# A hybrid decoder step: the first norm done by halves of the features, with the first products over the first half between

## The chip, the cores and the metric

The kernel runs on one core of a Trainium2 chip. The metric is the device time of one execution in microseconds (us), lower is better; a kernel's time is the median of several executions. A profile is one execution recorded by the hardware. The engines are PE (matrix products; PEld is its weight load), DVE (VectorE), ACT (ScalarE), POOL (GpSimd) and SP, which in this kernel only issues loads and stores. Each engine works through its own list of instructions in order.

## The reference

The kernel computes one step of a decoder of two layers, for 256 prompt tokens and 8 samples of 4 tokens, 288 tokens in all, with 1024 features. Layer 0 mixes by a gated delta rule, layer 1 by a Mamba-2 scan; each mixer is followed by a feed-forward block. All of this case happens ahead of the first mixer:

```python
cs = jax.nn.silu(c)                                   # 9 rows: one for the prompt, one for each sample
mod = cs @ p['w_mod'][i] + p['b_mod'][i]              # 1024 x 6144 weights per layer
sh1, sc1, gt1, sh2, sc2, gt2 = [m[:, None, :] for m in jnp.split(mod, 6, axis=-1)]
h = _rmsnorm(x, p['norm_mix'][i]) * (1 + sc1) + sh1   # x * rsqrt(mean(x*x) + eps) * weight
...
proj = h @ w_in                                       # q, k, v, z, and 32 columns beta_raw, a_raw
g = -exp(a_log) * softplus(a_raw + dt_bias)
cum = jnp.cumsum(g, axis=-1)                          # in chunks of 64 tokens
```

The outputs are the tokens after both layers and a final norm, and the states of the two mixers.

## The kernel before

Features lie on the partitions, in 8 tiles of 128 (index k), tokens along the free axis (288). Products are exact to fp32: activations and weights are each split into a high and a low part (`hh` and `hl`; `wh` and `wl`), and each feature tile takes three matmuls of 128x288: hh with wh, hh with wl, hl with wh. For weights, ACT makes `wh` as a copy with rounding and DVE makes `wl` as the difference (`chunk_load`, L267); a chunk is 4 feature tiles by 256 columns, 512 KB.

Loaded fp32 weights go through a pool of six tiles of 512 KB, tag "raw" (`raw_tile`, L141). It serves the conditioning weights and the product weights alike and is used in turn: a load takes the buffer of the sixth tile before it, and waits until the readers of that one are done. `wh` has four buffers and `wl` two. All loads are issued on SP in the order of its list.

The conditioning (`mod_steps`, L147) takes one slice of 1024 columns of w_mod in 8 loads of 128 rows. After every second load comes a burst of 8 matmuls, in which four column groups share one PSUM tile; after the last one ACT copies the sums (`mt`), PE transposes them in two pieces (`pt`), and DVE adds the bias and, for a scale, multiplies with the norm's weight (`modT`). A list `todo` holds all slices; `fill` and `ensure` take so many loads from it, and later stages weave the rest in between their work (`mods(8)` beside the first projections).

At the start (main body, L1584 on) the order is: c; two loads of w_mod; the bias and the norm weights; three tiles of x, with two loads of w_mod behind each of the first two; four loads more. Each x tile is transposed on PE and copied by DVE. Then comes the norm: ACT squares the tiles, DVE sums them (`acc`), two matmuls with ones give the mean (`ss`), ACT turns it into `rs` by a logarithm and an exponential, and DVE multiplies (`xr`). Constants of the convolutions and final norms (vr1 to vr3) are loaded and transposed. `ensure(2)` completes the slices of scale and shift, `load32` brings the 32 columns of beta and a, and `Norm.apply` makes `hh` and `hl`: first the 32 sample columns of all tiles (`hs`), then tile by tile a DVE step with scale and shift, an ACT copy to `hh` and a DVE difference to `hl`.

The mixer (`gdn`, L544) then computes the 32 columns (`dense32`, result `ba`), transposes them (`pb`), and forms beta and g: `gb` needs the bias `dtb`, which ACT's queue loads; softplus is an exponential on ACT (`spe`) and a row of small DVE steps (`spq`, `spp`); then `g`, and `pb` again as the cumulated sums, products with `triU`. Beside it run the projections of q and k by pairs of 128 columns (`k_pair`, L750; `dense_g`, L297): 48 matmuls a pair, evacuated by ACT (`ext`), followed by the convolution on DVE (`cva`, L72), and `kf`.

The order of each engine's list is fixed when the kernel is built, by a scheduler that works from the program's order and priorities.

Of the kernel before, what the change touches and what calls it, by code (L numbers as in the profile page):

```python
# [27 lines left out]
def tile_hybrid_step(ctx: ExitStack, tc: tile.TileContext, I, O):  # L28
# [45 lines left out]
    def tt(out, a, b, op):  # L74
        V.tensor_tensor(out=out, in0=a, in1=b, op=op)  # L75
# [99 lines left out]

    mod = {(l, s): const.tile([P, KD, 9], F32, name=f"modT{l}{s}") for l in range(2) for s in range(6)}
# [23 lines left out]
    class Norm:  # L200
# [22 lines left out]
        def apply(self, A, B, u=None, W=None, c0=0, at=()):  # L223

            r = None if u is not None else self.rstd()
            t = sqt("hs")[:, 0:256].rearrange("p (k t) -> p k t", k=KD)
            t4 = t.rearrange("p k (b t) -> p k b t", t=4)
            xs = (x if u is None else u)[:, :, NP_:NT].rearrange("p k (b t) -> p k b t", t=4)
            bc = lambda a: a[:, :, 1:9].unsqueeze(3).to_broadcast([P, KD, NB, 4])
            tt(t4, xs, bc(A), MUL)  # L230
            if u is None:
                tt(t, t, r[:, NP_:NT].unsqueeze(1).to_broadcast([P, KD, NS]), MUL)
            tt(t4, t4, bc(B), ADD)
            cp(hh[:, :, NP_:NT], t)
            tt(hl[:, :, NP_:NT], t, hh[:, :, NP_:NT].bitcast(F32), SUB)
            for k in range(KD):
                for i, a_ in enumerate(at):
                    if a_ == k:
                        load_early(W, c0, 4 * i, 4)
                if u is None:  # L240
                    v = sqt("hu")[:, 0:NP_]
                    stt(v, x[:, k, 0:NP_], A[:, k, 0:1], r[:, 0:NP_], MUL, MUL)
                    h = act(hh[:, k, 0:NP_], v, AF.Identity, bias=B[:, k, 0:1])
                    last = stt(hl[:, k, 0:NP_], v, B[:, k, 0:1], hh[:, k, 0:NP_].bitcast(F32), ADD, SUB)
                else:
                    v = u[:, k, 0:NP_]
                    ts(v, v, A[:, k, 0:1], B[:, k, 0:1], MUL, ADD)
                    cp(hh[:, k, 0:NP_], v)
                    tt(hl[:, k, 0:NP_], v, hh[:, k, 0:NP_].bitcast(F32), SUB)
            if u is None:  # L250
                self.after = [h, last]
# [123 lines left out]

    def dense32(W, c0, xh, xl):
        ps = psd.tile([P, NT], F32, tag="d", name="pd")
        whv, wlv = early.pop((c0, 32), None) or load32(W, c0)
        for k in range(KD):
            mm(ps, whv[:, k, :], xh[:, k, :], start=(k == 0), stop=False)  # L380
            mm(ps, wlv[:, k, :], xh[:, k, :], start=False, stop=False)
            mm(ps, whv[:, k, :], xl[:, k, :], start=False, stop=(k == KD - 1))
        return ps
# [160 lines left out]
    def gdn(gt1, nrm):  # L544
# [19 lines left out]
        pba = dense32(W, 6144, hh, hl)  # L564
# [168 lines left out]
        with tc.tile_pool(name="gp1", bufs=1) as p1:  # L733
# [17 lines left out]
            def k_pair(p_):  # L751
                ps = []
                yield from dense_g(ps, W, 1024 + p_ * 256, KD, hh, hl)
# [826 lines left out]
    queue_mods(0, (1, 0, 2, 3, 4, 5))  # L1580
    queue_mods(1, range(6))
    nrm = Norm()
    with tc.tile_pool(name="boot", bufs=1) as bp:
# [3 lines left out]
        act(cin, cin, AF.Silu)  # L1587
        pc = pm([P, KD, 32], "pc")
# [3 lines left out]
        fill(2)  # L1592
# [5 lines left out]
        for i, n in enumerate((P, P, NS)):  # L1598
            t = bp.tile([P, DM], F32, name=f"xt{i}")
            src = I["x_prompt"][0, i * P:(i + 1) * P, :] if i < 2 else I["x_sample"].rearrange("b t d -> (b t) d")  # L1600
            SY.dma_start(t[:n], src)
# [5 lines left out]
            if i < 2:  # L1607
                fill(2)
# [3 lines left out]
        fill(4)  # L1612
# [4 lines left out]
        for k in range(KD):  # L1617
            tt(xr[:, k, :], x[:, k, :], r, MUL)
        SY.dma_start(vr[1], I["gdn_conv_w"].rearrange("o w (r c) -> (o w r) c", c=P))
# [19 lines left out]
    nrm.apply(sc2, sh2, None, I["ffn_w_gate_up"][0], 0, (0,))  # L1639
# [40 lines left out]
    nrm.apply(sc1, sh1, None, I["ssm_w_in"][0], 4096, (0,))  # L1680
    nrm = Norm()
    ssm(gt1, nrm)
    nrm.apply(sc2, sh2, None, I["ffn_w_gate_up"][1], 0, (4,))
# [73 lines left out]
```

## Time and profile before

| | us |
|---|---|
| median of 3 runs | 1190.71 (1189.5 to 1194.89) |
| the profiled execution | 1194.17 |
| its span, first to last instruction | 1192.5 |
| PE busy | 1120.5 (94%) |
| DVE busy | 857.2 (72%) |
| ACT busy | 617.5 (52%) |
| DMA, mean over the span | 209 GB/s |

The mean granted clock of PE in the profiled execution was 0.972 of full speed. Times of the trace count from the span's start. In a chain of waits each row is a piece of the path that ended last, followed back from the last instruction. In a timeline a row gives start, length, engine, line, operation, output and inputs, and in brackets how long the engine had been idle and which instruction ended that. A group's row gives its count, busy time, mean ns of one, and the idle time ahead of it.

### The profile page before, as it was taken

The page shows a single profiled execution, that of the slowest core. Times are in us where ns is not written, and L with a number is a line of the kernel's source. Part 1 is how long each engine was busy: PE and PEld are TensorE (multiplying, and loading weights), DVE is VectorE, ACT ScalarE, POOL GpSimd, SP SyncE. Part 2 cuts the span into 40 slices and gives each one's busy share as a digit, 9 for nine tenths or more (in the row PEclk, how much of TensorE's full clock was granted, in tenths as well). Part 3 has the DMA queues.
Part 4 walks back from the last instruction along what each step waited for, and adds up shares of the span by engine and source line. Part 5 has one row for each costly group of instructions (what it writes and reads, how often), then busy time and mean ns, then how long its engine had stood idle before and what let it go on. Part 6 is the DMA issues. An engine that isn't in the chain of part 4 may idle for free.

```text
span 1192.5 us, 23174 instructions
## 1 busy us (share of the span) xinstructions
PE 1120.5 (94%) x8550; PEld 1022.6 (86%) x8550; DVE 857.2 (72%) x2080; ACT 617.5 (52%) x1315; POOL 120.9 (10%) x323
## 2 busy tenths in 40 slices
PE   5899999999989989999999899989979999999996
PEld 3689777798979879999999788768859899999996
DVE  2887897888767777666665777667876686666654
ACT  3587335555444464434343666887833484444432
POOL 3111104112100210100000111000000110000000
PEclk8999999899989989999999899999989989999998
DMA  8866696543354669888765767676464679887771
GB/s 301 258 205 179 187 290 189 174 150 105 103 173 152 206 205 315 271 273 266 240 196 157 255 204 235 192 226 202 147 208 146 190 227 302 256 254 232 216 215 51
DMA packets 270000, 249.04 MB, mean 209 GB/s; under 512 B 13314, under 2 KB 256247, under 8 KB 269888
## 3 DMA queue, kind: packets, MB, share of 16 engines
q1 hardware_dynamic: 269256, 247.51, 67.0%
q8 instruction: 67, 1.10, 0.4%
q14 instruction: 45, 0.37, 0.1%
q10 hardware_dynamic: 632, 0.07, 0.0%
HBM read 226.64 MB, written 20.90 MB: 208 GB/s over the span
## 4 chain that ended last, share of the span: by engine, by line
PE 72%; DVE 11%; DMA 8%; ACT 5%; issue 2%; POOL 1%; SPq 0%; DVEq 0%; ACTq 0%; POOLq 0%
PE pd L62 55%; PE pch L62 4%; DVE cva L72 3%; PE mod L62 3%; DVE wl L75 2%; DMA wm<-in_w_mod_dram 2%; DMA rw<-in_ssm_w_in_dram 1%; DMA rw<-in_gdn_w_in_dram 1%; ACT wh L87 1%; DMA D<-scumd 1%; PE py L62 1%; ACT D L82 1%; PE lsu L62 1%; PE pht L1431 1%; DMA rw<-in_gdn_w_out_dram 1%
## 5 line engine op out<-in xcount | busy, mean ns | idle before, releaser
L62 PE MATMUL pd<-hh,wh 128*128 128x288 f32 x1424 | 430.9, 305 | 13.8 <-ACT hh L87 10.4
L62 PE MATMUL pd<-hh,wl 128*128 128x288 f32 x1424 | 428.9, 302 | 4.6 <-DVE wl L75 4.3
L62 PE MATMUL pd<-hl,wh 128*128 128x288 f32 x1424 | 424.7, 300 | 1.2 <-DVE hl L72 1.0
L75 DVE TENSOR_TENSOR wl<-rw,wh 128x1024 fp32r<-128x1024 f32 (+2 forms) x258 | 310.7, 1204 | 153.7 <-PE pd L62 108.8
L87 ACT ACTIVATE wh<-rw 128x1024 fp32r<-128x1024 f32 (+2 forms) x258 | 268.1, 1041 | 251.5 <-PE pd L62 151.7
L62 PEld LDWEIGHTS pd<-hh,wh 128*128 128x128 f32 x1424 | 270.4, 191 | 27.5 <-issue 14.1
L62 PEld LDWEIGHTS pd<-hh,wl 128*128 128x128 f32 x1424 | 271.1, 190 | 11.0 <-DVE wl L75 8.1
L62 PEld LDWEIGHTS pd<-hl,wh 128*128 128x128 f32 x1424 | 270.4, 190 | 3.4 <-DVE hl L72 1.5
L62 PE MATMUL pd<-ah,wh 128*128 128x288 f32 x352 | 104.6, 297 | 0.0
L62 PE MATMUL pd<-al,wh 128*128 128x288 f32 x352 | 104.5, 297 | 0.0
L62 PE MATMUL pd<-ah,wl 128*128 128x288 f32 x352 | 104.1, 296 | 0.0
L72 DVE SCALAR_TENSOR_TENSOR cva<-ext,vT,cva 128x312 f32<-128x312 f32 x168 | 85.8, 535 | 10.2 <-ACT cva L82 9.4
L62 PEld LDWEIGHTS pd<-ah,wl 128*128 128x128 f32 x352 | 66.3, 188 | 0.0
L62 PEld LDWEIGHTS pd<-al,wh 128*128 128x128 f32 x352 | 66.2, 188 | 0.0
L62 PEld LDWEIGHTS pd<-ah,wh 128*128 128x128 f32 x352 | 66.1, 188 | 0.1
L62 PE MATMUL mod<-wm,csT 128*32 128x256 f32 x768 | 56.2, 419 | 8.1 <-DMA wm<-in_w_mod_dram 7.7
L62 PEld LDWEIGHTS mod<-wm,csT 128*32 128x32 f32 x768 | 21.8, 116 | 28.1 <-DMA wm<-in_w_mod_dram 9.0
L72 DVE SCALAR_TENSOR_TENSOR h0u<-h0u,elP,lsu 128x128 f32<-128x128 f32 x128 | 36.0, 341 | 7.6 <-PE lsu L62 6.2
L72 DVE SCALAR_TENSOR_TENSOR s0u<-s0u,elS,lu 128x128 f32<-128x128 f32 x128 | 36.3, 341 | 6.0 <-PE lu L62 6.0
L62 PE MATMUL pd<-ogh,wl 128*128 128x288 f32 x128 | 39.1, 305 | 1.3 <-DVE wl L75 1.3
L62 PE MATMUL pd<-ogh,wh 128*128 128x288 f32 x128 | 40.0, 314 | 0.0
L87 ACT ACTIVATE ext<-pd 128x256 f32<-128x256 f32 x112 | 27.5, 291 | 23.6 <-PE pd L62 21.9
(537 smaller groups left out, 1792.3 us busy)
## 6 DMA issues: line engine op xcount, KB each, us to landing
wm<-in_w_mod_dram SPq DMA_DIRECT2D x96, 512.0 KB
rw<-in_ffn_w_gate_up_dram SPq DMA_DIRECT2D x88, 512.0 KB
rw<-in_gdn_w_in_dram SPq DMA_DIRECT2D x48, 512.0 KB
rw<-in_ffn_w_down_dram SPq DMA_DIRECT2D x40, 512.0 KB
rw<-in_ssm_w_in_dram SPq DMA_DIRECT2D x40, 512.0 KB
s<-in_state_gdn_dram SPq DMA_DIRECT2D x16, 512.0 KB
rw<-in_gdn_w_out_dram SPq DMA_DIRECT2D x16, 512.0 KB
s0u<-in_state_gdn_dram SPq DMA_DIRECT2D x16, 512.0 KB
```

What stands on the lines that cost most here:

```text
L62: return T.matmul(out, lhsT=lhsT, rhs=rhs, start=start, stop=stop)
L72: return V.scalar_tensor_tensor(out=out, in0=a, scalar=s, in1=b, op0=o0, op1=o1)
L75: V.tensor_tensor(out=out, in0=a, in1=b, op=op)
L82: return S.activation(out=out, in_=a, func=f, bias=bias, scale=scale)
L87: S.activation(out=out, in_=a, func=AF.Copy)
L1431: T.transpose(pt[:, k, :], h0[:, o:o + P], ident)
```

## The change

x is loaded first, ahead of all conditioning weights. The first two slices of layer 0 (scale and shift) leave the list `todo` (`done[0] = 16` stands for them) and are done by a new function, `mod_half(s, h, m)`: one half of a slice, 512 columns, for four feature tiles. Four loads bring two row blocks each, 512 KB as before, in pieces of 2 KB where they were 4 KB; 8 matmuls of 128 columns follow each load, then one copy (`mth`), one transpose (`pth`) and the bias. `apply_half` does the norm's last step on four feature tiles.

```diff
+    def mod_half(s, h, m):
+        pmod = pss.tile([P, P], F32, tag="s", name=f"modh{s}{h}")
+        for k in range(0, KD, 2):
+            r = raw_tile(f"wh{s}{h}{k}").rearrange("p (k c) -> p k c", k=2)
+            SY.dma_start(r, I["w_mod"][0, k * P:(k + 2) * P, s * DM + 512 * h:s * DM + 512 * h + 512].rearrange(
+                "(k p) c -> p k c", p=P))
+            burst([lambda q=q, k=k, i=i, r=r: mm(pmod[32 * q:32 * q + 32, :], csT[:, k + i, :], r[:, i, q * P:(q + 1) * P],
+                                                 start=(k + i == 0), stop=(k + i == KD - 1))
+                   for i in range(2) for q in range(4)])
...
+        def apply_half(self, A, B, u, h):
...
+            for k in range(4 * h, 4 * h + 4):
+                v = u[:, k, 0:NP_]
+                ts(v, v, A[:, k, 0:1], B[:, k, 0:1], MUL, ADD)
+                cp(hh[:, k, 0:NP_], v)
+                tt(hl[:, k, 0:NP_], v, hh[:, k, 0:NP_].bitcast(F32), SUB)
...
+        mod_half(1, 0, mod[0, 1])
+        mod_half(0, 0, mod[0, 0])
+        early[6144, 32] = load32(W, 6144)
+        load_early(W, 1024, 0, 4)
+        ba32, ba_steps = dense32_g(W, 6144, hh, hl)
+        first = []
+        first_g = dense_g(first, W, 1024, KD, hh, hl)
+        nrm.apply_half(mod[0, 1], mod[0, 0], xr, 0)
+        next(ba_steps)
+        next(first_g)
+        next(first_g)
+        mod_half(1, 1, mod[0, 1])
+        mod_half(0, 1, mod[0, 0])
+        load_early(W, 1024, 4, 4)
+        nrm.apply_half(mod[0, 1], mod[0, 0], xr, 1)
+        next(ba_steps, None)
         SY.dma_start(vr[1], I["gdn_conv_w"].rearrange("o w (r c) -> (o w r) c", c=P))
...
-        ensure(2)
-        early[6144, 32] = load32(I["gdn_w_in"][0], 6144)
-        nrm.apply(mod[0, 1], mod[0, 0], xr, I["gdn_w_in"][0], 1024, ())
...
-    gdn(gt1, nrm)
+    gdn(gt1, nrm, ba32, first, first_g)
```

So over feature tiles 0 to 3 the products of the 32 columns (12 matmuls) and of the first K pair (24 matmuls, 12 for each of its two tiles) are written between the halves; `dense32_g` is `dense32` with a stop after tile 3, and `k_pair(0)` goes on where `first_g` was left. `Norm.apply` loses the branch that the first norm used. The loads, transposes and copies of vr1 to vr3 move behind the second half.

SP, the loads between x and the first K pair's second chunk. Before (`wm` is w_mod, the first `rw` the 32 columns, the others chunks of the first pair):

```order
L153 DMA wm_355<-in_w_mod_dram 128x1024
L153 DMA wm_365<-in_w_mod_dram 128x1024
L153 DMA wm_367<-in_w_mod_dram 128x1024
L365 DMA rw_383<-in_gdn_w_in_dram 128x8x32
L271 DMA rw<-in_gdn_w_in_dram 128x4x256
L153 DMA wm_641<-in_w_mod_dram 128x1024
L271 DMA rw<-in_gdn_w_in_dram 128x4x256
```

After (`wh_...` from L181 are halves of w_mod; wh_420 is the first load of the second half):

```order
L181 DMA wh_334<-in_w_mod_dram 128x2x512
L393 DMA rw_349<-in_gdn_w_in_dram 128x8x32
L299 DMA rw<-in_gdn_w_in_dram 128x4x256
L181 DMA wh_420<-in_w_mod_dram 128x2x512
L181 DMA wh_430<-in_w_mod_dram 128x2x512
L181 DMA wh_440<-in_w_mod_dram 128x2x512
L181 DMA wh_450<-in_w_mod_dram 128x2x512
L181 DMA wh_467<-in_w_mod_dram 128x2x512
L181 DMA wh_477<-in_w_mod_dram 128x2x512
L181 DMA wh_487<-in_w_mod_dram 128x2x512
L181 DMA wh_497<-in_w_mod_dram 128x2x512
L299 DMA rw<-in_gdn_w_in_dram 128x4x256
```

The product weights of the first half now stand ahead of the last eight loads of w_mod; before, all of w_mod's first two slices stood ahead of them.

PE, at the last conditioning products. Before:

```order
L62 MATMUL mod_274<-wm_355,csT 32x256 x4
L62 MATMUL mod_274<-wm_353,csT 32x256 x4
L62 MATMUL mod_274<-wm_367,csT 32x256 x4
L62 MATMUL mod_274<-wm_365,csT 32x256 x4
L167 MATMUL pt<-ident,mt 128x128 x2
L62 MATMUL pd<-hh,wh_385 128x288
```

After (the first three rows are the last of the 36 products over the first half):

```order
L62 MATMUL pd<-hh,wh 128x288
L62 MATMUL pd<-hh,wl 128x288
L62 MATMUL pd<-hl,wh 128x288
L62 MATMUL modh_419<-wh_430,csT 32x128 x8
L62 MATMUL modh_419<-wh_440,csT 32x128 x8
L62 MATMUL modh_419<-wh_450,csT 32x128 x8
L189 MATMUL pth<-ident,mth 128x128
L62 MATMUL modh_466<-wh_467,csT 32x128 x8
L62 MATMUL modh_466<-wh_477,csT 32x128 x8
L62 MATMUL modh_466<-wh_487,csT 32x128 x8
L62 MATMUL modh_466<-wh_497,csT 32x128 x8
L189 MATMUL pth<-ident,mth 128x128
```

Seven of the eight bursts of the second half stand behind all of the 36 products; the burst of wh_420 stands among them.

ACT, from `ba` to the softplus's exponential `spe`. Before:

```order
L555 DMA dtb<-in_gdn_dt_bias_dram 128x16
L556 DMA nea<-in_gdn_a_log_dram 128x16
L87 ACTIVATE ba<-pd 32x256
L87 ACTIVATE ba<-pd 32x128
L84 ACTIVATE junk,mh_587<-perm_580 128x128
L87 ACTIVATE hist<-ph 128x96
L84 ACTIVATE junk,mh_594<-perm_581 128x128
L87 ACTIVATE wh<-rw 128x1024
L82 ACTIVATE nea<-nea 128x16
L82 ACTIVATE spe<-spe 128x96
```

After:

```order
L87 ACTIVATE ba<-pd 32x256
L87 ACTIVATE ba<-pd 32x128
L593 DMA dtb<-in_gdn_dt_bias_dram 128x16
L594 DMA nea<-in_gdn_a_log_dram 128x16
L87 ACTIVATE ext_133<-pd 128x256
L84 ACTIVATE junk,mh_705<-perm_698 128x128
L87 ACTIVATE ext_133<-pd 128x8x4
L84 ACTIVATE junk,mh_712<-perm_699 128x128
L87 ACTIVATE ext_134<-pd 128x256
L87 ACTIVATE ext_134<-pd 128x8x4
L87 ACTIVATE hist<-ph 128x96
L82 ACTIVATE nea<-nea 128x16
L82 ACTIVATE spe<-spe 128x96
```

The two small loads moved behind `ba`, and the evacuation of the first K pair moved ahead of the exponential. On DVE, the convolution of that pair (six `cva` and two `kf`, where it was four `cva`) stands between `spq` and `g`. From about the 780th instruction of PE and the 219th of DVE on the two orders are the same.

More of the change, by code (lines that the diff above doesn't have):

```diff
@@ L174, in mod_steps @@
         yield
+    def mod_half(s, h, m):
[7 more added lines that the diff above has]
+                   for i in range(2) for q in range(4)])
+        mt = sqt("mth")[:, 0:P]
+        cp(mt, pmod)
+        pt = pm([P, P], "pth")
+        T.transpose(pt, mt, ident)
+        mv = m[:, 4 * h:4 * h + 4, :]
+        tt(mv, pt.rearrange("p (q r) -> p q r", q=4)[:, :, 0:9],
+           bmodT[:, 0, s, 4 * h:4 * h + 4].unsqueeze(2).to_broadcast([P, 4, 9]), ADD)
+        if s == 1:
+            stt(mv, mv, 1.0, nmix(0)[:, 4 * h:4 * h + 4].unsqueeze(2).to_broadcast([P, 4, 9]), ADD, MUL)
     mod = {(l, s): const.tile([P, KD, 9], F32, name=f"modT{l}{s}") for l in range(2) for s in range(6)}
@@ L239, in apply @@
                         load_early(W, c0, 4 * i, 4)
[L240 to L251, printed above, removed]
+                v = sqt("hu")[:, 0:NP_]
+                stt(v, x[:, k, 0:NP_], A[:, k, 0:1], r[:, 0:NP_], MUL, MUL)
+                h = act(hh[:, k, 0:NP_], v, AF.Identity, bias=B[:, k, 0:1])
+                last = stt(hl[:, k, 0:NP_], v, B[:, k, 0:1], hh[:, k, 0:NP_].bitcast(F32), ADD, SUB)
+            self.after = [h, last]
         @contextmanager
@@ L374, in load32, with dense32_g, steps @@
         return whv, wlv
-    def dense32(W, c0, xh, xl):
[L377 to L382, printed above, removed]
+    def dense32_g(W, c0, xh, xl):
+        ps = psd.tile([P, NT], F32, tag="d", name="pd")
+        def steps():
+            whv, wlv = early.pop((c0, 32), None) or load32(W, c0)
+            for k in range(KD):
+                mm(ps, whv[:, k, :], xh[:, k, :], start=(k == 0), stop=False)
+                mm(ps, wlv[:, k, :], xh[:, k, :], start=False, stop=False)
+                mm(ps, whv[:, k, :], xl[:, k, :], start=False, stop=(k == KD - 1))
+                if k == 3:
+                    yield
+        return ps, steps()
+    def dense32(W, c0, xh, xl):
+        ps, g = dense32_g(W, c0, xh, xl)
+        for _ in g:
+            pass
         return ps
@@ L542, in out_proj, with gdn @@
                             yield
-    def gdn(gt1, nrm):
+    def gdn(gt1, nrm, ba32, first, first_g):
         W = I["gdn_w_in"][0]
@@ L751, in k_pair @@
             def k_pair(p_):
-                ps = []
-                yield from dense_g(ps, W, 1024 + p_ * 256, KD, hh, hl)
+                ps = [] if p_ else first
+                yield from dense_g(ps, W, 1024 + p_ * 256, KD, hh, hl) if p_ else first_g
                 kf = []
@@ L1577, in late_ssm @@
                     SY.dma_start(O[8][0, 2 * bq + v, 16 * h2:16 * h2 + 16].rearrange("(k e) p n -> (e p) k n", e=2), hv[v])
-    queue_mods(0, (1, 0, 2, 3, 4, 5))
+    queue_mods(0, (2, 3, 4, 5))
+    done[0] = 16
     queue_mods(1, range(6))
@@ L1587, in tile_hybrid_step @@
         act(cin, cin, AF.Silu)
+        xts = []
+        for i, n in enumerate((P, P, NS)):
+            t = bp.tile([P, DM], F32, name=f"xt{i}")
+            src = I["x_prompt"][0, i * P:(i + 1) * P, :] if i < 2 else I["x_sample"].rearrange("b t d -> (b t) d")
+            SY.dma_start(t[:n], src)
+            xts.append((t, n))
         pc = pm([P, KD, 32], "pc")
@@ L1597, in tile_hybrid_step @@
         SY.dma_start(vr[0][112:128], I["norm_ffn"].rearrange("l (r c) -> (l r) c", c=P))
[L1598 to L1601, printed above, removed]
+        for i, (t, n) in enumerate(xts):
             for g in range(2):
```

30 lines of the change are left out of this document (17 added, 13 removed).

## The prediction

> **What bounds the kernel now.** I read the page first, for the time to work against, then the start of the program, since after about 140 us both kernels issue the same instructions in the same order. The page and the table by stages (columns: stretch, then busy us and count for PE, PEld, DVE, ACT, POOL, then granted clock, DMA share, GB/s):
>
> ```profile
> span 1192.5 us, 23174 instructions
> 5.00:20.00 15.00, 9.81 (x89) 5.87 (x93) 3.78 (x8) 3.02 (x5) 6.25 (x19) 1.00 1.03 394
> 20.00:31.00 11.00, 8.44 (x57) 3.65 (x53) 3.89 (x14) 6.06 (x12) 0.00 (x0) 0.54 0.86 293
> 31.00:38.00 7.00, 2.91 (x40) 1.34 (x33) 5.87 (x17) 3.57 (x9) 0.00 (x0) 0.99 1.03 329
> 38.00:47.00 9.00, 8.89 (x64) 7.73 (x63) 7.57 (x21) 5.53 (x17) 2.90 (x10) 0.81 0.70 227
> 47.00:62.00 15.00, 14.01 (x106) 13.08 (x105) 14.23 (x50) 7.72 (x22) 0.99 (x3) 1.00 0.69 223
> 62.00:80.00 18.00, 16.38 (x135) 14.08 (x134) 14.89 (x31) 14.53 (x47) 3.18 (x9) 1.00 0.78 245
> ```
>
> Until 38 us the kernel is bound by loads: the DMA share is about one while PE and ACT have room. From 47 us on it is bound by DVE (14.23 of 15 us) with PE close behind (14.01). The chain of waits (start, length, what) gives the joint between the two:
>
> ```profile
> 14.43 7.97 DMA wm<-in_w_mod_dram
> 22.54 1.97 PE mod L62 x16
> 24.52 9.28 DMA wm<-in_w_mod_dram
> 33.84 1.11 PE mod L62 x16
> 34.98 0.39 ACT mt L87
> 36.58 1.62 DVE xr L78 x5
> 38.97 3.34 DMA wm<-in_w_mod_dram
> 54.90 0.62 PE pb L62 x4
> 121.29 3.75 DMA rw<-in_gdn_w_in_dram
> ```
>
> The last conditioning load lands at 33.84; call that moment T. Everything of the mixer hangs on it: in the timelines of PE, ACT and DVE (start, length, engine, operation) the products start at 37.71, which is T + 3.87, and the gate chain of the mixer follows:
>
> ```profile
> 37.71 0.38 PE L62 MATMUL pd<-hh,wh 128*128 128x288 f32 x1 [1.86 <-ACT hh L87]
> 39.33 0.45 PE L62 MATMUL pd<-hh,wh 128*128 128x288 f32 x1
> 39.57 0.45 PE L62 MATMUL pd<-hh,wl 128*128 128x288 f32 x1
> 42.22 0.29 PE L62 MATMUL pd<-hh,wh 128*128 128x288 f32 x1
> 42.35 0.29 PE L62 MATMUL pd<-hh,wl 128*128 128x288 f32 x1
> 44.22 0.37 PE L571 MATMUL pb<-ident,ba 32*128 32x32 f32 x3
> 42.22 0.34 ACTq L555 DMA_DIRECT2D dtb<-in_gdn_dt_bias_dram  x1
> 43.22 0.53 ACT L87 ACTIVATE ba<-pd 32x256 f32<-32x256 f32 x2 [1.58 <-PE pd L62]
> 50.92 0.48 ACT L87 ACTIVATE ext<-pd 128x256 f32<-128x256 f32 x2 [0.46 <-PE pd L62]
> 44.77 0.21 DVE L75 TENSOR_TENSOR gb<-pb,dtb 128x48 f32<-128x48 f32 x1
> 46.78 0.21 DVE L78 TENSOR_SCALAR spq<-spe 128x96 f32<-128x96 f32 x1
> 54.65 0.19 DVE L75 TENSOR_TENSOR g<-gb,nea 128x48 f32<-128x48 f32 x1
> ```
>
> To be seen: products issue every 0.24 us at half clock (39.33 to 39.57) and every 0.13 at full clock (42.22 to 42.35); ba is out at 43.22, gb at 44.77, spq at 46.78, g at 54.65, and the cumulated sums (pb over triU) at 54.90, T + 21.06. The first pair of K tiles is evacuated at 50.92.
>
> **The change, part by part.** *x first.* Its three loads stand ahead of all of w_mod. Rows that price the norm:
>
> ```profile
> 11.87 0.69 DVE L1606 COPY x<-px 128x512 f32<-128x512 f32 x1 [6.56 <-PE px L1605]
> 21.14 0.77 ACT L82 ACTIVATE sq<-x 128x288 f32<-128x288 f32 x2
> 31.72 3.04 DVE L75 TENSOR_TENSOR xr<-x,rs 128x288 f32<-128x288 f32 x8 [4.43 <-ACT rs L82]
> 36.50 1.70 DVE L78 TENSOR_SCALAR xr<-xr,modT,modT 128x256 f32<-128x256 f32 x5
> 38.45 1.76 DVE L75 TENSOR_TENSOR hl<-xr,hh 128x256 fp32r<-128x256 f32 x5
> L75 DVE TENSOR_TENSOR wl<-rw,wh 128x1024 fp32r<-128x1024 f32 x5 | 6.1, 1222 | 0.3 <-ACT wh L87 0.3
> L87 ACT ACTIVATE wh<-rw 128x1024 fp32r<-128x1024 f32 x3 | 3.2, 1052 | 0.5 <-DMA rw<-in_gdn_w_in_dram 0.5
> L72 DVE SCALAR_TENSOR_TENSOR cva<-ext,vT,cva 128x312 f32<-128x312 f32 x6 | 3.2, 533 | 0.0
> L72 DVE SCALAR_TENSOR_TENSOR kf<-ext,cva 128x256 f32<-128x256 f32 x2 | 0.8, 422 | 0.0
> ```
>
> The first piece of x is copied at 11.87 now, behind sixteen mod products; with x first I estimate the sixth copy's end at 12.9. From the squares (21.14) to the normalised x (31.72) the chain takes 10.6 us, with other work between, so I put its start at 22.7 and its end 3.04 later, 25.7. The two first half slices are there by then: x and 4.2 MB at the 394 GB/s of the first stage take 14 us, from about 5. So this edit frees the products from x and leaves T to w_mod.
>
> *First-half products.* From xr to the first product stand two sample steps, wl of the small weight, a scaled tile (1.70 / 5 = 0.34) and its copy, about 1.8 us: first product at 27.5, ten us before 37.71. ACT casts the chunk (1.05) between the first and second feature tile and DVE splits it (1.22), up to about 29.8; the 7 products that need neither are done, 29 are left. At 0.13 us they would end at 33.6, at 0.24 at 36.8; with half clock for the first 3.6 us (as from 37.71 to 41.3 now) 7 go by 31.5, and 22 more take 2.9: 34.4.
>
> *The new wait.* Raw tiles have 6 buffers, and their order of use is now: 8 first-half loads, small weight, chunk, 8 second-half loads, chunk. The fifth second-half load (wh_467) takes the small weight's buffer, the sixth (wh_477) that of the chunk and so waits for DVE's wl at about 31, and the eighth (wh_497) that of the second (wh_430), whose matmuls stand on PE behind all 36 products. SP stands still for each, with the second chunk and the convolution constants queued behind. So the last load goes out at 34.4 plus about 0.4 of matmuls. A load alone took 3.34 and 3.75 us in the chain; streamed at 394 GB/s it is 1.33. It is alone here but for wh_487 ahead of it, so I take 3.34: the new T is 38.2, with bounds of 36.1 (1.33) and 40.9 (the 0.24 us products and 3.75). Against 33.84 it is 4.4 late: w_mod's last byte no longer comes as the queue can bring it, because its buffer waits for the products put between. Pieces of 2 KB in place of 4 KB I cost at nothing: the last bytes wait for a buffer, not for the rate; were all 16 loads some 5% slower, the first eight would land half a us later, under the norm.
>
> *After T.* Half as many matmuls and a smaller copy: the first product at T + 3.3, not T + 3.87. DVE then has four scaled tiles (1.36), wl (1.22), the sample split and four hl (0.35 each): the last hl near T + 6.1, ba at T + 6.5, pb at T + 7.2, where before it was T + 10.4. What was gained there is lost at two places on ACT, which runs in order. The bias dtb is now issued behind ba's copies, where it stood ahead of them; issue at 42.22 to use at 44.77 bounds that load by 2.55, so gb comes at T + 9.6 (before T + 10.9). The exponential of the softplus now stands behind all four ext copies of the pair. The pair has 24 products left beside ba's 12, the first 15 at half clock: 3.6 + 2.8 = 6.4, done at T + 9.7; copies, history, nea and the exponential bring spq to T + 11.6 (before T + 12.9).
>
> From spq to g takes 7.9 us now, DVE never idle. In the new order two more cva (533 ns) and two kf (422 ns) stand in that stretch, 1.9 us: g at T + 21.4, the sums at T + 21.7, say 22 with the moved copies of the constants. That is 60.2, 5.3 later than 54.90. Given back: PE has 109 products done there where it had 98, 11 x 0.13 = 1.4, and DVE the 1.9 us of cva and kf. The rest is the same order, so 5.3 - 1.9 = 3.4 by DVE; some of it is taken up where loads are late (121.29), and I take **+3**. Break-even is a T near 35. The profiled execution took 1194.17 us, 1.67 over its span and 3.5 over the median of 1190.71; so 1197.2 for such an execution, and 1193.7 on the median.
>
> [...]
>
> **The rivals.** *Slower: clock.* All 36 products of the first half at half clock, as the 0.54 of 20 to 31 us allows: their end is 36.8, T = 40.6. PE then idles some 4 us, and if its second 36 all go at 0.24, the pair ends at T + 11.9 and spq at T + 13.8 = 54.4, where 46.78 was: 7.6 late, plus 1.9 of cva and kf, less the same given back: +7.6, 1198.3. It decides from T = 40 on. For it: PE is thinly used there, with chunk and hl waits between. Against: before, 3.6 us of products brought the full clock back. [...] Chance 0.23.
>
> *Faster: the lead stands.* If wh_497 lands at 36.1 and ACT's copies cost less than I think, the pair ends at T + 9.7 = 45.8, not 50.92, and the 36 products taken out of the stage from 38 us (36 x 0.13 = 4.7) stay gained: -5, 1185.7, and -7 with T at 34.6. For it: PE is 14.01 of 15 busy behind T, so its work moved ahead is worth something. Against: DVE is the busier there, and its first waiter, g, moves with T. Chance 0.17.
>
> *No change: the front is covered.* The lag ends in a later stretch bound by loads:
>
> ```profile
> DMA  8866696543354669888765767676464679887771
> ```
>
> The sixth slice, 149 to 179 us, has 9; loads for it are issued as buffers come free, so a late start is partly made up there. Time 1190 to 1192. Against: buffers come free by the products, which are late. Chance 0.15. That the products don't stand between the halves is excluded by PE's new order.
>
> **How the numbers follow.** Forecast 0.45, at 1193.7; slower rival 0.23; faster 0.17; covered 0.15. A measurement of this kernel can tell about 0.5%, 6 us: faster is below 1184.8, slower above 1196.7. Of the faster rival half reaches so far, with a little for unknown gains: 0.12. Of the slower one nearly all, 0.21, with 0.05 from the forecast's upper end (T at 39.5 and more): 0.26. Same: 0.62. Range: the low end leaves out the better half of the faster rival, 1186.5; the high end takes in the clock rival and leaves out a T of 40.9 with every product cold, 1200.
>
> **What would show it.** Right: SP standing before the last w_mod load until about 35 us, its landing at 38 or later, DMA share well under one from 31 to 38, PE idle for 3 us and more there, 36 products before it, gb some 2.4 us behind pb, the exponential behind the pair's copies, the sums at 58 to 62 us. Wrong: a landing before 36 us, or the sums before 55; a clock of 0.5 in both halves would make it the slower rival; and a difference that arises after 140 us would be none of these.

## The result and the profile after

The changed kernel takes 1207.02 us in the median of 4 runs (1201.42 to 1211.35), the kernel before 1192.80 us on the same chip (1189.5 to 1196.19): a ratio of 1.0108 (95% interval 1.0076 to 1.0139). It is slower, by about 13 us by the ratio (14 between the medians), where 3 were forecast. The profiled execution of after took 1211.35 us and is its slowest; its mean clock is 0.964, before had 0.972. The page's head and its row of DMA shares, and the stages that the prediction shows of before:

```profile
span 1209.6 us, 23440 instructions
DMA  8756498453353569988766768677554579888761
5.00:20.00 15.00, 9.22 (x101) 7.58 (x102) 6.55 (x14) 7.19 (x14) 6.25 (x19) 0.98 1.06 360
20.00:31.00 11.00, 7.35 (x91) 5.34 (x90) 8.29 (x24) 5.40 (x11) 0.00 (x0) 0.66 0.84 277
31.00:38.00 7.00, 6.60 (x82) 6.05 (x85) 0.01 (x1) 0.28 (x1) 0.00 (x0) 0.86 0.47 156
38.00:47.00 9.00, 6.11 (x79) 4.91 (x78) 5.56 (x17) 2.76 (x7) 0.00 (x0) 0.79 0.85 265
47.00:62.00 15.00, 11.69 (x68) 9.97 (x68) 10.09 (x32) 6.79 (x20) 2.81 (x13) 0.73 0.73 242
62.00:80.00 18.00, 17.99 (x135) 16.07 (x134) 12.21 (x41) 10.33 (x36) 3.06 (x8) 0.95 0.70 212
```

From 31 to 38 us PE works on the first products where it had room before (6.60 us against 2.91), and the loads fall off: share 0.47, where it was 1.03. What was gained there is lost behind it: in 47 to 62 us PE is 11.69 of 15 us busy where it was 14.01, at a clock of 0.73 where it was 1.00. PE's timeline, from the first product to the cumulated sums (last row of the first part), and then two rows near 100 us:

```profile
27.52 0.58 PE L62 MATMUL pd<-hh,wh 128*128 128x288 f32 x1 [3.25 <-ACT hh L87]
35.49 0.29 PE L62 MATMUL pd<-hl,wh 128*128 128x288 f32 x1
40.35 0.64 PE L62 MATMUL modh<-wh,csT 128*32 128x128 f32 x16 [0.95 <-DMA wh<-in_w_mod_dram]
41.45 0.33 PE L189 MATMUL pth<-ident,mth 128*128 128x128 f32 x1 [0.46 <-ACT mth L87]
43.57 0.61 PE L62 MATMUL pd<-hh,wh 128*128 128x288 f32 x1 [0.99 <-ACT hh L87]
48.99 0.42 PE L609 MATMUL pb<-ident,ba 32*128 32x32 f32 x2
55.51 0.54 PE L62 MATMUL pd<-hh,wh 128*128 128x288 f32 x2 [1.86 <-ACT wh L87]
57.49 0.61 PE L62 MATMUL pd<-hh,wl 128*128 128x288 f32 x1 [1.45 <-DVE wl L75]
65.55 0.61 PE L62 MATMUL pb<-triU,g 128*16 128x128 f32 x4
...
99.23 0.53 PE L62 MATMUL pd<-hh,wh 128*128 128x288 f32 x2 [1.38 <-ACT wh L87]
100.90 0.40 PE L62 MATMUL pd<-hh,wl 128*128 128x288 f32 x1 [1.13 <-DVE wl L75]
```

The first product starts at 27.52, ten us before the 37.71 of before. The 36th ends at 35.8. SP's row of the second half's eight loads:

```profile
21.68 15.11 SPq L181 DMA_DIRECT2D wh<-in_w_mod_dram  x8
```

The last of them goes out at 36.4, behind the products and the burst whose buffer it takes. PE waits for it until 40.35, and the shift's last transpose comes at 41.45 (before: 35.42). From there every step is late, up to the sums at 65.55 (54.90). ACT's and DVE's timelines in the same stretch:

```profile
48.16 0.53 ACT L87 ACTIVATE ba<-pd 32x256 f32<-32x256 f32 x2 [3.73 <-PE pd L62]
49.52 0.34 ACTq L593 DMA_DIRECT2D dtb<-in_gdn_dt_bias_dram  x1
53.26 0.28 ACT L82 ACTIVATE spe<-spe 128x96 f32<-128x96 f32 x1
54.41 1.04 ACT L87 ACTIVATE wh<-rw 128x1024 fp32r<-128x1024 f32 x1
52.61 0.21 DVE L75 TENSOR_TENSOR gb<-pb,dtb 128x48 f32<-128x48 f32 x1 [2.04 <-DMA dtb<-in_gdn_dt_bias_dram]
53.58 0.21 DVE L78 TENSOR_SCALAR spq<-spe 128x96 f32<-128x96 f32 x1
56.22 1.22 DVE L75 TENSOR_TENSOR wl<-rw,wh 128x1024 fp32r<-128x1024 f32 x1
62.41 0.21 DVE L75 TENSOR_TENSOR g<-gb,nea 128x48 f32<-128x48 f32 x1
```

`gb` waits 2.04 us for the bias whose load is issued behind `ba`. The next pair's chunk is cast (`wh`) only at 54.41, behind the exponential and ACT's steps of the first pair's convolution, and split (`wl`) at 56.22: the two stands of PE before 55.51 and 57.49 end with these two.

To see where the lag arises I set the start of the nth product (all `pd` matmuls, in order) beside that of before, from the two traces; positive is late:

```
product          0     25    50    75    125   200   250   300    550    1200
before, us      37.7   43    48    51    61    76    85    94    144    327
after, lag     -10.2  -8.7  -0.4  +6.8  +8.4  +5.6  +10.8 +13.9  +13.7  +14.7
```

The lead of ten us is gone by the 50th product, seven us are lost by the 75th, and about eight more between the 200th and the 300th. From there to the 3600th (740 us, +13.2) nothing is added. This execution, the slowest of four, loses 4 us more between 755 and 1020 us, at a granted clock of 0.95 there, 0.97 before; in the median run that is not to be expected. The second loss is read from SP's timeline, of after and then of before:

```profile
78.91 0.34 SPq L153 DMA_DIRECT2D wm<-in_w_mod_dram  x1
89.73 0.28 SPq L490 DMA_DIRECT2D out_dram<-hc  x1
92.47 2.06 SPq L299 DMA_DIRECT2D rw<-in_gdn_w_in_dram  x4
```

```profile
73.34 2.21 SPq L271 DMA_DIRECT2D rw<-in_gdn_w_in_dram  x2
81.70 0.28 SPq L452 DMA_DIRECT2D out_dram<-hc  x1
```

In after the first group of history stores stands right behind the conditioning load at 78.91, and SP waits for their data until 89.73; four chunk loads stand behind them and go out at 92.47. Before, two of these loads stood ahead of the stores. PE then idles for ACT's cast and DVE's split at 99.23 and 100.90.

### The profile page after: what moved, and what is told of

It reads as the page before. It is cut to its first block, busy times and chain, and to the rows that moved or that the text cites. A ratio compares the mean times of both kernels' runs of the same rounds, so it can differ in the third digit from the quotient of the medians.

```text
span 1209.6 us, 23440 instructions
## 1 busy us (share of the span) xinstructions
PE 1131.3 (94%) x8678; PEld 1036.9 (86%) x8678; DVE 858.3 (71%) x2086; ACT 618.1 (51%) x1318; POOL 120.6 (10%) x323
## 4 chain that ended last, share of the span: by engine, by line
PE 68%; DVE 9%; DMA 6%; ACT 4%; issue 2%; SPq 0%; POOL 0%; DVEq 0%; ACTq 0%; POOLq 0%
PE pd L62 52%; PE pch L62 4%; PE mod L62 2%; DVE cva L72 2%; DMA D<-scumd 2%; DVE wl L75 1%; DMA rw<-in_ssm_w_in_dram 1%; PE py L62 1%; DMA rw<-in_gdn_w_in_dram 1%; ACT D L82 1%; ACT wh L87 1%; DMA rw<-in_ffn_w_gate_up_dram 1%; PE pht L1469 1%; PE lsu L62 1%; PE pst L62 1%
## 5 line engine op out<-in xcount | busy, mean ns | idle before, releaser
L62 PEld LDWEIGHTS pd<-hh,wh 128*128 128x128 f32 x1424 | 272.3, 192 | 34.3 <-issue 16.2
L62 PEld LDWEIGHTS pd<-hh,wl 128*128 128x128 f32 x1424 | 274.3, 193 | 13.0 <-DVE wl L75 9.7
L62 PEld LDWEIGHTS pd<-hl,wh 128*128 128x128 f32 x1424 | 273.8, 193 | 1.9 <-DVE hl L72 0.7
L62 PE MATMUL mod<-wm,csT 128*32 128x256 f32 x640 | 44.8, 403 | 3.8 <-DMA wm<-in_w_mod_dram 3.8
L521 POOL COPY cvo<-ext 128x27 f32<-128x27 f32 x56 | 21.4, 384 | 206.4 <-ACT ext L87 206.1
L82 ACT ACTIVATE ext<-cva 128x312 f32<-128x312 f32 x56 | 25.6, 460 | 31.7 <-DVE cva L72 30.8
```

Of the source, the lines that this page charges most:

```text
L62: return T.matmul(out, lhsT=lhsT, rhs=rhs, start=start, stop=stop)
L82: return S.activation(out=out, in_=a, func=f, bias=bias, scale=scale)
L521: G.tensor_copy(o[:, c % 4, 0:27].rearrange("p (n s) -> p n s", s=3), e[:, 256:319].rearrange("p (n s) -> p n s", s=7)[:, :, 0:3])
```

## The experiments

Each run below is a ratio to the kernel before, timed on the same chip. The lags are those of the one profiled execution of each kernel, at products 75, 300 and 1200, so a difference of a few us between two rows may be chance; "transpose" is the shift's last one, "sums" the start of the cumulated sums.

| run | transpose | sums | 75 | 300 | 1200 | ratio (95%) |
|---|---|---|---|---|---|---|
| after | 41.45 | 65.55 | +6.8 | +13.9 | +14.7 | 1.0108 (1.0076 to 1.0139) |
| e1_own_tiles | 40.45 | 65.79 | +7.5 | +13.8 | +14.7 | 1.0090 (1.0063 to 1.0117) |
| e2_products_behind | 41.45 | 66.81 | +8.5 | +14.8 | +15.4 | 1.0127 (1.0099 to 1.0155) |
| e3_late_stores | 42.17 | 65.45 | +8.0 | +10.6 | +14.0 | 1.0115 (1.0087 to 1.0143) |
| e4_early_bias | 43.56 | 64.91 | +9.1 | +15.3 | +16.7 | 1.0154 (1.0125 to 1.0183) |
| e5_next_chunk | 41.55 | 65.17 | +2.0 | +13.6 | +14.7 | 1.0092 (1.0068 to 1.0116) |
| e6_first_store_late | 41.83 | 64.82 | +7.5 | +8.9 | +16.2 | 1.0096 (1.0066 to 1.0126) |
| e7_chunk_and_store | 40.92 | 64.10 | +1.1 | +9.6 | +17.8 | 1.0128 (1.0097 to 1.0160) |
| e8_x_first_alone | 35.50 | 55.13 | +0.4 | +0.2 | +0.7 | 0.9989 (0.9967 to 1.0011) |
| e9_halves_alone | 40.26 | 62.27 | +5.0 | +6.4 | +10.1 | 1.0102 (1.0075 to 1.0130) |
| e10_products_last | 35.23 | 60.93 | -0.1 | +5.5 | +3.6 | 1.0034 (1.0020 to 1.0049) |
| e11_last_and_chunk | 35.58 | 61.14 | -1.4 | +2.7 | +7.4 | 1.0051 (1.0027 to 1.0074) |
| e12_last_shared_tiles | 38.19 | 64.13 | +3.1 | +6.6 | +7.1 | 1.0068 (1.0050 to 1.0087) |
| e13_last_and_bias | 38.64 | 59.38 | +3.8 | +9.7 | +10.4 | 1.0080 (1.0053 to 1.0108) |
| e14_last_and_vr | 41.19 | 63.97 | +4.3 | +3.1 | +7.2 | 1.0072 (1.0055 to 1.0088) |
| e15_idle_filled | 41.67 | 66.30 | +9.6 | +13.8 | +14.2 | 1.0146 (1.0120 to 1.0171) |
| e16_idle_filled_more | 42.57 | 64.49 | +8.0 | +10.8 | +13.0 | 1.0103 (1.0081 to 1.0125) |
| e17_last_bias_between | 37.71 | 59.91 | +2.8 | +8.3 | +9.1 | 1.0058 (1.0034 to 1.0082) |
| e18_filled_bias_between | 42.42 | 59.67 | +9.1 | +10.2 | +10.5 | 1.0089 (1.0054 to 1.0125) |

### The buffers, and the products' place as written (e1, e2)

e1 gives the second half tiles of its own, so that its loads wait for no reader; nothing is moved in any engine's order.

```diff
-            r = raw_tile(f"wh{s}{h}{k}").rearrange("p (k c) -> p k c", k=2)
+            t = own.tile([P, 1024], F32, name=f"wo{s}{k}") if own else raw_tile(f"wh{s}{h}{k}")
+            r = t.rearrange("p (k c) -> p k c", k=2)
...
-        mod_half(1, 1, mod[0, 1])
-        mod_half(0, 1, mod[0, 0])
+        mod_half(1, 1, mod[0, 1], bp)
+        mod_half(0, 1, mod[0, 0], bp)
```

> The second half's eight conditioning loads get tiles of their own, so the last one no longer waits for the buffer of the load whose matmuls stand behind the 36 products; the order of every engine stays as in the changed kernel. Theory 1 (the lag is a sum: the shift's second half is late, PE then starves between the pair and the cumulated sums, and SP stands before the stores of the convolution history): the last load lands some 7 us earlier, near 33 us, but the seven bursts still stand behind the 36 products, so the shift's transpose (41.45 in the changed kernel, 35.42 before) comes only about 1 us earlier and the time falls by 1 us, to about 1.010 of before. Theory 2 (the buffer wait is the lag, as the prediction had it): the time falls by 4 to 7 us, to about 1.005 of before. Theory 3 (the lag is PE's half clock, about 90 us of half-clock time against 68): the time follows the half-clock time and not the landing.

PE's timeline of e1 behind the 36 products:

```profile
38.04 1.96 PE L62 MATMUL modh<-wo,csT 128*32 128x128 f32 x64
40.45 0.33 PE L190 MATMUL pth<-ident,mth 128*128 128x128 f32 x1 [0.46 <-ACT mth L87]
```

The loads are all there: the shift's four bursts (64 matmul instructions in the trace) run without a wait. Yet the last transpose is only 1.0 us earlier than in after. With the buffers out of the way the second half is held by something else, almost as long: seven of its eight bursts stand on PE behind the 36 products. The buffer wait of the prediction is there, but it is not the only one. The time is the same as after's within the intervals.

e2 writes the 36 products behind the second half's function (the three `next` calls move down two lines).

> The 36 products over the first half are written behind the second half's conditioning, loads and all else as in the changed kernel; only PE's order moves, by some twenty rows. Theory 1: the shift's transpose comes about 3 us earlier (38 to 39 us) and the time falls by about 3 us, to 1.008 of before. Theory 2: the buffer wait is gone as well, since the readers no longer stand behind the products, so 4 to 7 us, 1.005. Theory 3: no change unless the half-clock windows near 43 and 57 us go.

The scheduler still puts most of them ahead of the bursts, since their inputs are ready first; the last transpose stays at 41.45. This run tells nothing on the place; e10 and e12 do.

### The waits downstream, one by one (e3 to e7)

e3 puts off each group's history stores by one group. (Two groups share a tile there, so what it stores is the history of a later group.) e6 holds back those of the first group alone, in a tile of their own.

```diff
...
+                if self.held == []:
+                    self.held = [(g, ot)]
+                    return
...
```

> The stores of each group of the convolution history are issued when the next group is done, so SP no longer stands for 10.8 us (78.9 to 89.7 us) with four chunk loads behind the stores; the start up to 66 us stays as in the changed kernel. Theory 1: the lag at 127 us falls from 14.4 to about 10 us, the time by 3 to 4 us, to 1.008 of before. Theory 2: these loads were covered: no change, 1.011. Theory 3: only the half-clock windows at 88 and 101 us go, at most 2 us.

> The changed kernel with the stores of the first group of the convolution history alone issued with those of the second group, all later stores as they are. Theory 1: SP's standing from 78.9 to 89.7 us goes, two chunk loads pass it, the lag at 127 us falls from 14.4 to about 10 us and stays there: 1.008 of before. Rival: what is gained there is lost again behind it, as when all stores were put off (10.8 us of lag up to 780 us, then 13.9): 1.011.

e4 loads the gates' constants at the program's start; e5 loads the next pair's chunk, `load_early(W, 0, 0, 4)`, before the constants of the convolution; e7 is e5 with e6.

> The two small gate constants are loaded at the program's start, not on ACT behind the copies of ba; the scheduler then also puts the softplus's exponential ahead of the pair's evacuation. Theory 1: gb no longer waits 2 us, the chunk casts behind the exponential come earlier, PE's standing of 3.3 us at 53 to 57 us shrinks, the cumulated sums come at 61 to 63 us in place of 65.55, and the time falls by 3 us, to 1.008 of before. Theory 2: the sums come earlier but PE's products don't: no change. Theory 3: less standing, so no fall to half clock at 57 us: 3 us as well.

> The changed kernel with the first weight chunk of the second pair loaded and split right behind the last products of ba, so that ACT and DVE cast it while the first pair runs (in the changed kernel they cast it at 54.4 and 56.2 us, behind the pair's evacuation, and PE's lag grows from -0.4 us at the 50th product to +6.8 at the 75th). Theory 1, revised after the runs on the load's buffer and on the products' place changed nothing: this standing is most of the loss; the lag at the 75th product falls to 2 to 4 us and the time by about 4 us, to 1.007 of before. Theory 2: the gate chain on DVE sets the pace (g at 62.4 us in the changed kernel), so the cumulated sums stay at 65 us and the time at 1.011. Theory 3: only the half clock that follows the standing goes, 1 to 2 us.

> Both edits of the two kernels before in one. Theory 1: the two losses are separate and their gains add up: 8 us, 1.004 of before. Theory 2: one of them is covered by the other: no more than the better of the two alone, 1.007.

Each of these waits goes or shrinks when its cause is removed, and none of the five kernels is faster than after by more than the intervals. With the chunk early (e5) the lag at the 75th product falls from 6.8 to 2.0 us, and is 13.6 again at the 300th. With the first stores late (e6) the step of 8 us between the 200th and the 300th product is halved (from 4.9 to 8.9, where after goes from 5.6 to 13.9), and 7 us are lost between the 300th and the 1200th. e4 takes the wait for the bias away (`gb` starts at 52.35 without one), but with the small loads at the program's start the norm's mean (`ss`) comes at 22.07 in place of 18.71 and the first product 2.9 us later (30.41). The time grows, so e4 does not price the bias alone. Together the five suggest that these waits are where the lag shows, not what makes it.

### The change in parts (e8, e9)

e8 is the kernel before with x loaded first; e9 has the norm by halves, but the first products written inside the mixer, as before.

> The kernel before with one part of the change alone: x is loaded ahead of w_mod, all else as before. Theory 1: the last conditioning load still lands near 34 us, since all the bytes ahead of it are the same, and the time is that of before within 2 us, 0.999 to 1.002. Rival: the norm's end at 35 us counted too, and the time falls by 2 to 4 us.

> The norm by halves as in the changed kernel, but the first products are written where they were before (inside the mixer), not between the halves. PE's list still has 28 of the 36 ahead of most of the second half's bursts, because the scheduler takes what is ready, and ACT and DVE have the order of the changed kernel up to 66 us; but SP's list has its two chunk loads ahead of the stores of the convolution history again, as before. Theory 1 (a loss of 10 us at the front, of which the late second half is the start, and one of 4 us at SP's stores): the sums at 65 to 66 us, the lag at 127 us 9 to 10 in place of 14.4, the end 1.008. Rival (writing the products early is the loss): 1.002. Rival (the front alone decides, SP's stores are covered): 1.011.

The sums in e8's timeline of PE, 0.23 us later than before:

```profile
55.13 0.61 PE L62 MATMUL pb<-triU,g 128*16 128x128 f32 x4 [0.43 <-DVE g L75]
```

x first costs and gains nothing. e9 loses as much as after. In its order, too, the scheduler puts products between the halves (first product 27.49), and the last transpose is at 40.26. Two chunk loads stand ahead of the history stores there, as before, and the lag does not step up at them (6.3 us at the 200th product, 6.4 at the 300th). So the time of after is lost without that step as well.

### The products held behind the conditioning (e10, e12, e11)

e10 has e1's own tiles, and an order edge: the 36 products may not be issued on PE before the shift's last transpose `tr`.

```diff
...
+        mod_half(1, 1, mod[0, 1], bp)
+        tr = mod_half(0, 1, mod[0, 0], bp)
+        with tc.issue_after(tr.ins):
+            next(ba_steps)
+            next(first_g)
+            next(first_g)
```

> All 36 products over the first half are held behind the shift's last transpose on PE, and the second half's loads have tiles of their own, so the 16 conditioning loads stream and each burst runs when its load lands; all else as in the changed kernel. Theory 1 (PE's 36 products at mostly half clock, 27.5 to 35.5 us, hold up the second half's bursts): the shift's last transpose at 34 to 36 us in place of 41.45, the sums at 57 to 60 in place of 65.55, the time 1.004 to 1.006, as SP still stands at the stores. Rival: the front's loss is the standing and the half clock behind the pair, which this leaves: 1.009 to 1.011.

Two rows of PE and two of DVE in e10:

```profile
34.12 0.64 PE L62 MATMUL modh<-wo,csT 128*32 128x128 f32 x16 [0.85 <-DMA wo<-in_w_mod_dram]
35.23 0.33 PE L190 MATMUL pth<-ident,mth 128*128 128x128 f32 x1 [0.46 <-ACT mth L87]
48.08 0.21 DVE L75 TENSOR_TENSOR gb<-pb,dtb 128x48 f32<-128x48 f32 x1 [1.93 <-DMA dtb<-in_gdn_dt_bias_dram]
60.68 0.20 DVE L75 TENSOR_TENSOR g<-gb,nea 128x48 f32<-128x48 f32 x1
```

The last burst waits for its load again, the transpose is where it was before (35.23 against 35.42), and 9 of the 13 us are back: 1.0034, an interval clear of after's. SP still stands ahead of the stores in e10, from 71.1 to 79.6 us with four chunk loads behind them, and the lag still steps up there, from -2.0 us at the 200th product to 5.5 at the 300th. With e9 this says that the stand at the stores is not what decides the time. One thing moves along with the edge: the scheduler now puts the next chunk's cast ahead of the exponential (48.43 in e10, 54.41 in after; the same order in e12). e5, which brought that chunk forward alone, was no faster. e12 is e10 without the tiles of its own.

> As the kernel with the products held back, but the second half's loads share the six raw tiles as in the changed kernel: what is undone is the products' place on PE alone. Theory 1 (the place on PE is the loss, the buffers only follow it): the sixth load of the second half still waits for the chunk's split near 30 us, so the shift's last transpose comes at 36 to 37 us, 1 to 2 us later than with own tiles, and the time is 1.004 to 1.006 of before. Rival (own tiles were needed as well): the transpose at 38 us or later, 1.008 or more.

```profile
35.17 1.08 PE L62 MATMUL modh<-wh,csT 128*32 128x128 f32 x16 [1.67 <-DMA wh<-in_w_mod_dram]
38.19 0.47 PE L189 MATMUL pth<-ident,mth 128*128 128x128 f32 x1 [0.46 <-ACT mth L87]
```

The bursts wait for loads again, with the products out of their way. The transpose comes 3.0 us later than e10's, and the ratio, 1.0068, is 3.4 thousandths higher, 4 us. So the place on PE, with the orders that move along with it, is worth about 5 us and the shared buffers about 4, which e1 could not show because the products still stood in the way. (The first share is the less certain: e12's interval, up to 1.0087, reaches into after's, from 1.0076.) e11 adds e5's early chunk to e10.

> The kernel with the products held back and own tiles, and the second pair's first chunk loaded and split behind ba as well; in this kernel's SP list three chunk loads stand ahead of the stores of the convolution history. Theory 1: the three losses (late second half, standing behind the first pair, SP at the stores) are all of it: the sums at 57 to 59 us, the lag at 127 us under 4, the time 0.999 to 1.003. Rival: something else holds the stages behind 140 us back as soon as the order differs, as when the first stores were put off: 1.006 or more.

The lag at the 300th product is 2.7 in place of 5.5, and at the 1200th 7.4 in place of 3.6: again a wait removed at one place comes back at a later one.

### What is left: gate constants, clock (e13 to e18)

e13 is e10 with the gate constants at the program's start, e14 is e10 with the convolution's constants loaded ahead of the conditioning as before, e17 is e10 with `dtb` and `nea` issued behind the last conditioning copy.

> The kernel with the products held back and own tiles, with the gate constants loaded at the start; ACT then has the softplus's exponential ahead of the second evacuation of the pair, and DVE has one cva and both kf of the pair behind g. Theory 1 (what is left of the loss there, 3 to 5 us, is the gate chain: g at 60.7 us against 54.6 before): g at 55 to 57 us, the sums at 56 to 58, the time 0.999 to 1.002. Rival (what is left is SP's standing at the stores, which stays): 1.003 or more.

> The kernel with the products held back and own tiles, with the convolution constants loaded and transposed ahead of the conditioning, as before the change; the scheduler then issues dtb ahead of ba's copies and the exponential ahead of the pair's evacuation, two chunk loads stand ahead of SP's stores, but g stays behind all six cva and two kf. Theory 1: gb about 2 us earlier, g at 57 to 59 us, SP's standing gone: 0.999 to 1.002. Rival (g's place behind the convolution is what counts): 1.003 or more.

> The kernel e10 (products held behind the shift's last transpose, own tiles for the second half), with the two small loads dtb and nea issued on ScalarE's queue right behind the last conditioning copy (34.8 us) and no longer behind ba (45.6). Theory that what is left of the loss comes of the gate chain: in e10 dtb landed at 48.1, 1.9 us after its first reader stood ready, and was issued where chunk loads fill the queues; now it is there when pb is done, gb at 46.1, and with the exponential's row of small steps ahead of the pair's convolution g comes at 57 to 58 in place of 60.7: ratio 1.000 to 1.002. Rival, that the rest comes of VectorE's convolution and of the stores ahead of the chunk loads at 80 to 94 us: gb early, but the ratio stays at 1.003 to 1.005.

PE's sums in e17:

```profile
59.91 0.61 PE L62 MATMUL pb<-triU,g 128*16 128x128 f32 x4
```

The sums come earlier than in e10 in e13 and e17 (59.38 and 59.91 against 60.93), and the time does not follow: 1.0080 and 1.0058. In each of the three the conditioning itself ended later (38.64, 41.19, 37.71 against 35.23), so they don't isolate the constants.

e15 and e16 are the changed kernel with matmuls that nobody reads in PE's idle places: 4, 8 and 14 of them in e15, 8, 12 and 26 in e16. The other engines' orders in e15 are those of after.

```diff
+    def warm(after, n):
...
+        with tc.issue_after(after.ins):
+            for _ in range(n):
+                mm(wt[0], ident, ones)
```

> The changed kernel with 26 matmuls more, whose results nobody reads, in the places where TensorE stands idle in the profile after: 4 ahead of the last conditioning burst, 8 behind the last transpose of the shift (41.45), 14 behind the first gate slice's burst (52.57 to 53.64). The lists of all other engines are the same. Theory clock: the half clock from 43 to 50 us and from 57 to 64 us comes of those idle stretches; with them filled the clock stays full, some 24 and 26 products go at 0.13 in place of 0.24 us (2.6 and 2.9 us), and the kernel is some 4 to 6 us faster than the changed kernel: about 1202, a ratio of 1.006. Theory waits: TensorE runs ahead of ScalarE's casts and VectorE's differences there anyway, so that a fuller clock only makes it wait longer: the half clock is gone but the time is the changed kernel's, 1207, ratio 1.011. If the half clock stays, the run tells nothing on this.

> As the run before it, with 8, 12 and 26 matmuls in place of 4, 8 and 14, for the case that the smaller number doesn't keep the clock up. By the clock theory the ratio is 1.006 to 1.008 (the larger filling may hold products back by about 1 us); by the theory of waits 1.011 or more.

The stages by clock, of after and of e15 (columns as above, the clock third from the end), then, under those of e15, one row of DVE and one of PE:

```profile
36.00:43.00 7.00, 4.28 (x115) 3.00 (x103) 1.83 (x8) 1.60 (x4) 0.00 (x0) 1.00 0.74 227
43.00:50.00 7.00, 6.43 (x25) 5.55 (x25) 4.43 (x13) 1.96 (x8) 0.45 (x1) 0.51 0.83 262
57.00:64.00 7.00, 6.51 (x28) 6.50 (x29) 6.80 (x26) 2.23 (x4) 0.46 (x1) 0.52 0.94 328
```

```profile
36.00:43.00 7.00, 6.14 (x133) 5.17 (x128) 1.62 (x7) 1.57 (x4) 0.00 (x0) 1.00 0.71 214
43.00:50.00 7.00, 6.38 (x45) 5.51 (x45) 5.19 (x16) 2.10 (x9) 1.88 (x8) 1.00 0.65 197
57.00:64.00 7.00, 4.36 (x20) 4.13 (x21) 6.96 (x20) 2.58 (x4) 0.00 (x0) 0.76 0.88 297
55.16 0.21 DVE L87 TENSOR_TENSOR gb<-pb,dtb 128x48 f32<-128x48 f32 x1 [6.09 <-DMA dtb<-in_gdn_dt_bias_dram]
57.99 0.40 PE L64 MATMUL pd<-hh,wh 128*128 128x288 f32 x1 [2.75 <-ACT wh L99]
```

The clock was full from 43 to 50 us (1.00), `ba` a us earlier (47.21 for 48.16), and no time came of it (1.0146). Over the whole profiled execution the mean clock was 0.975 in e15 and 0.974 in e16, above the 0.972 of before, where after had 0.964. The bias, though issued earlier (48.02 for 49.52), landed later, so that `gb` waited 6.09 us at 55.16 and with it everything behind it on DVE. e18 is e16 with the bias issued behind the last conditioning copy.

> The kernel e16 (idle places of TensorE filled, the products still between the halves), with the same two loads issued right behind the last conditioning copy. In e16 the clock was full from 43 us on, but gb waited 3.97 us for dtb and stopped VectorE's list, so that the sums came as late as before the filling. Theory that clock and this load share the loss, each hiding the other: with both removed gb comes at 49.7 in place of 54.0, the sums at 61 to 62 in place of 64.5, and the ratio falls to 1.005 to 1.008. Rival, that the late conditioning (last transpose at 42.6) alone holds the loss: sums at 64, ratio 1.010.

```profile
59.67 0.61 PE L64 MATMUL pb<-triU,g 128*16 128x128 f32 x4
```

The sums come 5 us earlier than in e16, and the ratio is 1.0089, an interval that overlaps after's and e16's. The 26 matmuls added behind the gate slice's burst (6.07 us in e16's trace) may hold its products back (+9.1 at the 75th); by how much isn't settled.

## Why the prediction was right and wrong

The direction of the lag was right, its size was not: +3 us forecast, about +13 measured. Step by step:

- **First product at 27.5** (27.52), x first worth nothing (e8), the **bias behind ba** and the **exponential behind the pair's copies**: as forecast. So are the 2 KB pieces, costed at nothing: in e10, where the sixteen loads stream, the last one is in use at 34.12 (33.84 before).
- **T = 38.2.** It was 40.3, inside the bounds, and by the path that the prediction named: the products ended at 35.8, not 34.4, the last load went out at 36.4, not 34.8, and took 3.9 us to its first reader, not 3.34.
- **PE idle for 3 us and more from 31 to 38 us: wrong.** PE is 6.60 of 7 us busy there, and waits 0.95 us for the last load, up to 40.35. "The new wait" was put on the buffer of the eighth load alone; e1 shows that taking this wait away gives 1.0 us at the transpose. The bursts that the prediction itself saw on PE behind the 36 products have no term in its sum, beyond the 0.4 us of the one whose buffer is waited for. e10 and e12 price the two: about 5 us for the place and what moves with it, about 4 for the buffers.
- **After T, +22.** The sums came at T + 25.2. The steps up to `ba` took the half clock throughout (0.52 from 43.0 to 48.2 us): `pb` stood at T + 8.6, not T + 7.2, `gb` at T + 12.3, not T + 9.6, `g` at T + 22.1 against T + 21.4. From `g` to the sums it was 3.1 us, where the sum had some 0.6: PE still had products ahead of them, until 63.6 at half clock (0.50 from 57.5 to 63.6). So the sums were 10.7 us late where 5.3 were forecast; 2.1 of the difference is T, 0.7 the way to `g`, and 2.5 the way from there.
- **"Given back: 1.9 us" and "the rest is the same order": the step that failed most.** The terms stopped at the sums and took 1.9 us off for products and convolution done early. In fact nothing was given back: the lead of the products was spent by the 50th, and the lag of 10.7 us at the sums was 13.9 at the 300th product. In after's trace it shows at the next chunk, cast and split behind the pair's convolution (7 us by the 75th product), and at SP's list, which the change had rearranged as far as the stores at 79 to 92 us (8 us up to the 300th). The prediction did not follow SP's list beyond the first pair.
- **The slower rival, clock,** happened in part: T of 40.3 is where it decides, and two stretches ran at 0.51 and 0.52. But e15 and e16 show that it is not the cause of the loss by itself: with a mean clock above that of before the loss stayed, and DVE then waited longer for the bias (6.09 us in e15). What their added matmuls cost is not separated from this.

What the runs show: the six kernels that hold the products behind the conditioning lie at 1.0034 to 1.0080, and after with the eleven others that have halves at 1.0089 to 1.0154; the two groups' intervals overlap. Within the first group the ratio rises with the time of the last transpose, from e10 and e11 (35.23, 35.58) over e17 and e12 (37.71, 38.19) to e13 (38.64). e14 is the exception: its transpose comes at 41.19, nearly as late as after's, and its ratio is 1.0072. So most of the loss, 9 of the 13 us between after and e10, goes with the products' place and the shared buffers, which make the second half of the conditioning late, but that lateness alone does not set the time. That the later waits (chunk, bias, stores) only pass the lag on is what e3 to e7, e9 and e10 suggest; which of them ends last in which stage changes from kernel to kernel. Not settled is the rest of 4 us in e10: the gate chain there is 6 us late at the sums, but e13 and e17 brought the sums forward without a gain. None of the versions beat the kernel before; e8, which has no halves, equals it.

## What to carry to other kernels

Work that is ready early is no gain where it stands, on an engine that runs in order, ahead of the readers of data that everything later waits for (here the shift's transpose came at 41.45 us in after and at 35.23 in e10); price its place in the list, not only its duration, and try it with an order edge before believing a buffer. When a change leads an order written by a scheduler into new rows, compare the load and store list to its end, not only to the first joint: here it differed as far as the stores at 79 to 92 us. Removing the wait that a trace shows is a test of that wait: if the time stays, something else sets it, and the lag may only have been passed on.

## What the runs showed of the hardware

The half clock came here without one long wait. In after, the stretch from 36 to 43 us has PE 4.28 of 7 us busy, its longest idle pieces there are 0.95 and 0.99 us (the second ends at 43.57), and the next 7 us go at 0.51; with the idle places partly filled (e15: 6.14 of 7 us busy) they go at 1.00. So in after a thinly used stretch was enough. In before, where 20 to 31 us ran at 0.54, PE's longest idle piece from 9 to 31 us is 1.30 us.

An 8 KB load took between 2.5 and 7.1 us from its issue to its use. `dtb` was waited for in all three: issued at 45.56 and used at 48.08 in e10, 3.1 us before its use at 52.61 in after, and 7.1 us before in e15 (issue at 48.02, use at 55.16). In e15 three 512 KB loads had been issued in the two us before it, in e10 none for more than six; that they are what held it up is not shown by itself.
